# A causal mask moved from TensorE to VectorE in a two-layer decoder trunk

## The chip, the core and the metric

The program runs on one core of a Trainium2 chip. The metric is the device time of one execution in microseconds (us). Three runs of the kernel before gave 2209.25, 2209.4 and 2209.67 us; their median is 2209.4 us. The engines are named as in the profile: PE is TensorE's matrix products, PEld its weight loads, DVE is VectorE, ACT is ScalarE, POOL is GpSimd, SP is the engine that issues most of the transfers.

## What is computed

Two layers over 256 tokens of width 2048, in float32. Each layer has a token mixer (one input projection that feeds eight heads of differential attention, an RG-LRU and a gated linear attention, then one output projection) and a SwiGLU feed-forward part. The part that matters here is the attention:

```
s = jnp.einsum('bhmqd,bhmkd->bhmqk', q_blk, kh)          # m = 0, 1: two score maps per head, d = 64
qpos = i * Q_BLOCK + jnp.arange(Q_BLOCK)                 # Q_BLOCK = 128
s = jnp.where(kpos[None, :] <= qpos[:, None], s, -jnp.inf)
p = jax.nn.softmax(s, axis=-1)
a = p[:, :, 0] - lam * p[:, :, 1]
return jnp.einsum('bhqk,bhkv->bhqv', a, vh)
```

## The kernel before

Weights stream from HBM through a ring of five `raw` tiles. Each 128x512 weight chunk is split into a high and a low part, `hilo`, by ACT (a rounding copy) and DVE (a subtraction). Every projection is then made of three products for each chunk and token half (`block`, lines 419 to 421): activation high times weight high, high times low, low times high. In the trace the products of the input projection are `in`. These run one after the other nearly without a break from the start of the kernel to its end.

Everything else (attention, LRU, gated linear attention) is written as Python generators that a planner, `Lane`, weaves in between those products. The planner keeps a clock, `lane.clk`, that is advanced by an estimated time for each product, and one such estimate for DVE and ACT each (`dve.free`, `act.free`: for DVE 0.1 us and 1.04 ns for each element of a row). A generator yields a time to wait, a tile tag that must be free, and a condition; its next instructions are written into the program when the planner's clock says that they will be ready. So the order of instructions on each engine is fixed when the program is built, and the estimates decide it; at run time each engine goes through its list in order and waits on semaphores.

The attention of head `h` in a group `g` of four heads and query tile `qt` (0 or 1) is `head(h)` inside `attention`. In order: two score products for m = 0 and 1 into `sps` (line 875; their contraction is 64 long and lies on partitions 0 to 63 for m = 0 and 64 to 127 for m = 1; each writes a PSUM bank of its own; 128 keys for `qt` 0, 256 keys for `qt` 1). Behind each of them a product of a bf16 identity `ident_b` with a bf16 tile `cmask` (0 on and under the diagonal, -1e30 above it) that accumulates the mask onto the 128 columns of the diagonal (line 877). Then DVE takes the row maximum `nm` of both maps, ACT the exponential `e` with its row sum, DVE three small steps and the difference of the maps, PE transposes it (`tpa`, line 902), ACT copies it to `aT`, PE multiplies by the values (`po`, line 912). The tag `sc`, of which there is one, is held from the score products to the exponential. Two layers, two groups, two query tiles and four heads make 32 such heads in all, 64 score products and 64 mask products. An fp32 product is two passes on PE, so that a score product is two rows of MATMUL.

Further products that the trace shows and that are of use here: `psa` (line 1106, in the gated linear attention) is a set of four fp32 products with contraction 64 and 128 columns that alternate between partitions 0 to 63 and 64 to 127 and between two PSUM banks, followed by `in` products; `psg` (line 976) is two fp32 products with contraction 128 and 256 columns. DVE and ACT operations are all recorded under line 173, the planner's helper.

Of the kernel before, what the change touches and what calls it, by code (L numbers as in the profile page):

```python
# [10 lines left out]
F32 = mybir.dt.float32  # L11
F32R = mybir.dt.float32r
BF16 = mybir.dt.bfloat16
# [3 lines left out]
ALU = mybir.AluOpType  # L17
AX = mybir.AxisListType

P = 128  # L20
# [167 lines left out]
def after(us):  # L188
    return (us, None, None)
# [3 lines left out]
def tile_hybrid_trunk(ctx, tc, x, xT, w_in, w_out, w_gu, w_down, post_norms, lams,  # L193
                      vecs, wbd, w_gup, ropes, out):
    nc = tc.nc
    PS = bass.MemoryType.PSUM
    lane = Lane()
    done = lane.done
    dve, act = Engine(lane, nc.vector, 0.1, 1.04e-3), Engine(lane, nc.scalar, 0.1, 0.83e-3)
# [10 lines left out]
    cst = ctx.enter_context(tc.tile_pool(name="cst", bufs=1))  # L210
# [9 lines left out]
    rope = cst.tile([P, 2, NT, 64], F32, tag="rope", name="rope")  # L220
    ident = cst.tile([P, P], F32, tag="ident", name="ident")
    make_identity(nc, ident)
    ident_b = cst.tile([P, P], BF16, tag="identb", name="ident_b")
    nc.gpsimd.tensor_copy(ident_b, ident)
    cmask = cst.tile([P, P], BF16, tag="cmask", name="cmask")
    nc.gpsimd.memset(cmask, 0.0)
    nc.gpsimd.affine_select(out=cmask, in_=cmask, compare_op=ALU.is_ge, fill=NEG, base=0,
                            pattern=[[-1, P]], channel_multiplier=1)
# [329 lines left out]
    def split_scaled(hi, lo, src, scale):  # L558

        if scale is None:  # L560
            act.copy(hi, src)
            dve.tensor_tensor(out=lo, in0=src, in1=hi.bitcast(F32), op=ALU.subtract)
        else:
            act.activation(hi, src, AF.Copy, scale=scale)
            dve.scalar_tensor_tensor(out=lo, in0=src, scalar=scale, in1=hi.bitcast(F32),
                                           op0=ALU.mult, op1=ALU.subtract)

    def turned(src, tag, name):

        if tag == "sc":  # L570
            tp = pp.tile([P, 2, 512], F32, tag="sc", name=name, bufs=1)[:, 0, :]
        else:
            tp = pp.tile([P, 512], F32, tag=tag, name=name, bufs=1)
        tp = tp.rearrange("p (c t) -> p c t", c=4)
        for c in range(4):
            nc.tensor.transpose(tp[:, c, :], src[:, c * P:(c + 1) * P], ident)
        lane.clk += 0.44
        return tp
# [7 lines left out]
    def wide(name, tag="rp"):  # L586
        return pm.tile([P, 512], F32, tag=tag, name=name, bufs={"rp": 3, "e": 2, "on": 1}[tag])
# [154 lines left out]
    for l in range(DEPTH):  # L742
# [93 lines left out]
        def rows(name, *needs):  # L836

            return small(name, *needs).rearrange("p a b -> p (a b)").rearrange("p (t n) -> p t n", t=NT)
# [18 lines left out]
        def attention(g, qt):  # L857


            nk = (qt + 1) * P  # L860
            rsum = pt.tile([P, 4, 2], F32, tag="rsum", name="rsum")
            ssq = pt.tile([P, 4], F32, tag="ssq", name="ssq")
            po = []

            def head(h):
                prev = (l, g, qt, h - 1) if h else (l, g, 0, 3) if qt else (l, g - 1, 1, 3)
                yield 0.3, None, lane.has((l, "q", g), (l, "k", g), (l, "v", g), (l, "small"), (prev, "s"))
                yield 0.0, "sc", lambda: lane.use["e"] < 2
                done[(l, g, qt, h), "s"] = True
                lane.use["e"] += 1  # L870
                qT, kT, v = tiles[l, "q", g], tiles[l, "k", g], rows((l, "v", g))
                sps = pp.tile([P, 2, 512], F32, tag="sc", name="sps", bufs=1)
                for m in range(2):
                    r0 = slice(64 * m, 64 * m + 64)
                    nc.tensor.matmul(sps[:, m, :nk], qT[r0, h, qt * P:(qt + 1) * P],
                                     kT[r0, h, :nk], start=True, stop=False)
                    nc.tensor.matmul(sps[:, m, qt * P:nk], ident_b, cmask, start=False, stop=True)
                lane.clk += 0.55 if qt == 0 else 0.98
                yield after(0.3)
                nm = pt.tile([P, 2], F32, tag="nm", name="nm")  # L880
                dve.tensor_reduce(out=nm, in_=sps[:, :, :nk], axis=AX.X, op=ALU.max, negate=True)
                yield dve.through()
                e = wide("e", "e").rearrange("p (m k) -> p m k", m=2)
                esum = pt.tile([P, 2], F32, tag="esum", name="esum")
                for m in range(2):
                    act.activation(e[:, m, :nk], sps[:, m, :nk], AF.Exp, bias=nm[:, m:m + 1],
                                         accum_out=esum[:, m:m + 1])
                act.drops("sc")
                yield act.through()
                dve.reciprocal(rsum[:, h, :], esum)  # L890
                yield NOW
                ncf = pt.tile([P, 1], F32, tag="ncf", name="ncf")
                dve.scalar_tensor_tensor(out=ncf, in0=esum[:, 0:1], scalar=nlam,
                                               in1=rsum[:, h, 1:2], op0=ALU.mult, op1=ALU.mult)
                yield NOW
                dve.scalar_tensor_tensor(out=e[:, 0, :nk], in0=e[:, 1, :nk], scalar=ncf,
                                               in1=e[:, 0, :nk], op0=ALU.mult, op1=ALU.add)
                yield dve.through(W_SM, "tr", lambda: lane.use["aT"] < 2)
                lane.use["aT"] += 1
                tp = pp.tile([P, 2, P], F32, tag="tr", name="tpa", bufs=1)  # L900
                for kt in range(qt + 1):
                    nc.tensor.transpose(tp[:, kt, :], e[:, 0, kt * P:(kt + 1) * P], ident)
                lane.use["e"] -= 1
                lane.clk += 0.11 * (qt + 1)
                aT = pt.tile([P, 2, P], F32, tag="aT", name="aT", bufs=2)
                act.copy(aT[:, :qt + 1, :], tp[:, :qt + 1, :])
                act.drops("tr")
                yield act.through(W_AT, ("o" if h == 0 else None), lane.has((prev, "av")))
                if h == 0:
                    po.append(pp.tile([P, 4, P], F32, tag="o", name="po", bufs=1))  # L910
                for kt in range(qt + 1):
                    nc.tensor.matmul(po[0][:, h, :], aT[:, kt, :], v[:, kt, h * P:(h + 1) * P],
                                     start=(kt == 0), stop=(kt == qt))
                lane.use["aT"] -= 1
                done[(l, g, qt, h), "av"] = True
                lane.clk += 0.22 * (qt + 1)
                yield after(0.3)
                junk = pt.tile([P, 512], F32, tag="junk", name="junk", bufs=1)[:, :P]
                act.activation(junk, po[0][:, h, :], AF.Square, accum_out=ssq[:, h:h + 1])
                yield act.through()  # L920
                done[(l, g, qt, h), "end"] = True

            def norm():
                yield 0.0, None, lane.has(*(((l, g, qt, h), "end") for h in range(4)))
                r0sq = pt.tile([P, 4], F32, tag="r0sq", name="r0sq", bufs=2)
                dve.tensor_tensor(out=r0sq, in0=rsum[:, :, 0], in1=rsum[:, :, 0], op=ALU.mult)
                rr = pt.tile([P, 4], F32, tag="rr", name="rr", bufs=2)
                yield NOW
                yield from rsqrt(rr, ssq, 4, 1.0 / P, pre=r0sq)
                dve.tensor_tensor(out=rr, in0=rr, in1=rsum[:, :, 0], op=ALU.mult)  # L930
                yield NOW
                on = wide("on", "on")
                dve.tensor_tensor(out=on.rearrange("p (h d) -> p h d", h=4), in0=po[0],
                                        in1=rr[:, :, None].to_broadcast([P, 4, P]), op=ALU.mult)
                dve.drops("o")
                yield dve.through(0.25, "tr")
                tp = turned(on, "tr", name="tpo")
                sl = slice(qt * P, (qt + 1) * P)
                split_scaled(yh[:, 4 * g:4 * g + 4, sl], yl[:, 4 * g:4 * g + 4, sl], tp, subw)
                dve.drops("tr")  # L940
                done[l, "y", g, qt] = True

            done[(l, -1, 1, 3), "s"] = done[(l, -1, 1, 3), "av"] = True
            for h in range(4):
                lane.add(10 + 2 * g + qt + h / 8, head(h))
            lane.add(9, norm())
# [555 lines left out]
```

## Time and profile before

| | |
|---|---|
| median of 3 runs | 2209.4 us |
| the profiled execution | 2209.7 us |
| its span, first to last instruction | 2208.0 us |
| PE busy | 2182.3 us, 99% of the span |
| DVE busy | 1801.3 us, 82% |
| ACT busy | 1368.3 us, 62% |
| mean rate of the transfers | 212 GB/s |
| granted TensorE clock, mean | 0.999 |

A row of the timeline gives the start, the duration, the engine, the line, the operation, what it writes and reads, the shape and a count. Where rows of one kind follow without idle time they are merged: `x2` with 0.48 us means that the first began and the last ended 0.48 us apart. PE's rows overlap, since matmuls are pipelined: an `in` product has a row of 0.39 us, and the next one starts 0.22 us behind it. What a product takes from the engine is therefore read from the distance between ends (start plus duration) of neighbours and not from its own duration.

### The profile page before, as it was taken

Reading aid. Unit: us, or ns where it says so; the run is one execution under the profiler, and the core shown is the slowest. Engines: PE = TensorE matmul, PEld = TensorE weight load, DVE = VectorE, ACT = ScalarE, POOL = GpSimd, SP = SyncE. Lnnn points to the kernel's source line nnn. Section 1 sums busy time; section 2 is a strip of 40 time slices with the busy share of each in tenths; the row PEclk is TensorE's granted clock in tenths of the full one; section 3 lists DMA queues with packets and bytes.
Section 4 is the critical chain, followed back from the end, with each engine's and each line's share of the span. In section 5 each row is a group of like instructions: output and inputs, shape, how many; then the busy total and the mean of one; then the engine's idle time right before and its main releaser. Section 6 shows DMA issues by size and latency. Waiting matters only on the chain.

```text
span 2208.0 us, 30990 instructions
## 1 busy us (share of the span) xinstructions
PE 2182.3 (99%) x10116; PEld 1782.8 (81%) x10116; DVE 1801.3 (82%) x3341; ACT 1368.3 (62%) x2713; POOL 96.2 (4%) x129
## 2 busy tenths in 40 slices
PE   8999999999999999999999999999999999999998
PEld 7777878887888888888877778788878888888886
DVE  6666865898999999999786668658989999999985
ACT  6455755776666666666564557556666666666663
POOL 0000000000000000000000000000000000000000
PEclk9999999999999999999999999999999999999999
DMA  8553646677877777777644537466777887777774
GB/s 289 183 156 105 197 162 217 198 224 222 252 246 240 240 242 237 243 234 247 216 149 150 171 92 217 156 216 200 221 231 244 250 250 239 240 235 242 235 240 138
DMA packets 202722, 467.32 MB, mean 212 GB/s; under 512 B 16416, under 2 KB 27200, under 8 KB 202560
## 3 DMA queue, kind: packets, MB, share of 16 engines
q1 hardware_dynamic: 186880, 434.93, 59.5%
q0 software_dynamic: 15104, 29.37, 7.9%
q8 instruction: 79, 1.29, 0.2%
q10 hardware_dynamic: 576, 1.05, 0.1%
q14 instruction: 83, 0.68, 0.1%
HBM read 463.18 MB, written 2.10 MB: 211 GB/s over the span
## 4 chain that ended last, share of the span: by engine, by line
PE 90%; DVE 6%; DMA 1%; ACT 1%; issue 1%; SPq 0%; DVEq 0%; ACTq 0%
PE in L419 6%; PE down L419 6%; PE down L421 6%; PE in L421 6%; PE down L420 6%; PE in L420 6%; PE gu_q L456 5%; PE gu_q L455 5%; PE gu_q L454 5%; PE gu_p L454 5%; PE gu_p L456 5%; PE gu_p L455 5%; DVE hilo L173 3%; PE op L419 3%; PE op L421 3%; PE op L420 3%
## 5 line engine op out<-in xcount | busy, mean ns | idle before, releaser
L173 DVE TENSOR_TENSOR hilo<-raw,hilo 128x512 fp32r<-128x512 f32 (+1 forms) x1472 | 954.4, 675 | 288.0 <-ACT hilo L173 283.2
L173 ACT CAST hilo<-raw 128x512 fp32r<-128x512 f32 (+1 forms) x1472 | 853.9, 614 | 274.8 <-PE gu_x L456 65.4
L173 ACT CAST hilo<-t 128x512 fp32r<-128x512 f32 x384 | 231.2, 621 | 151.2 <-DVE t L173 103.4
L419 PE MATMUL in<-hilo,hh 128*128 128x512 f32 (+1 forms) x768 | 301.0, 392 | 6.0 <-ACT hilo L173 6.0
L421 PE MATMUL in<-hilo,hl 128*128 128x512 f32 (+1 forms) x768 | 287.6, 374 | 0.8 <-DVE hl L173 0.8
L420 PE MATMUL in<-hilo,hh 128*128 128x512 f32 (+1 forms) x768 | 287.0, 374 | 0.6 <-DVE hilo L173 0.6
L419 PE MATMUL down<-hilo,hid 128*128 128x512 f32 x704 | 276.9, 393 | 4.4 <-DVE c_c L173 3.6
L421 PE MATMUL down<-hilo,hid 128*128 128x512 f32 x704 | 274.7, 390 | 1.0 <-DVE hid L173 1.0
L420 PE MATMUL down<-hilo,hid 128*128 128x512 f32 x704 | 274.2, 389 | 0.0
L173 DVE TENSOR_TENSOR hilo<-t,hilo 128x512 fp32r<-128x512 f32 x384 | 247.8, 684 | 2.6 <-ACT hilo L173 2.2
L419 PEld LDWEIGHTS in<-hilo,hh 128*128 128x128 f32 x768 | 145.3, 189 | 30.8 <-ACT hilo L173 6.4
L456 PE MATMUL gu_q<-hilo,hl 128*128 128x512 f32 x432 | 168.2, 389 | 0.0
L454 PE MATMUL gu_q<-hilo,hh 128*128 128x512 f32 x432 | 168.2, 389 | 0.0
L455 PE MATMUL gu_q<-hilo,hh 128*128 128x512 f32 x432 | 168.2, 389 | 0.0
L421 PEld LDWEIGHTS in<-hilo,hl 128*128 128x128 f32 x768 | 144.6, 188 | 27.4 <-DVE hl L173 1.3
L420 PEld LDWEIGHTS in<-hilo,hh 128*128 128x128 f32 x768 | 145.3, 189 | 22.5 <-DVE hilo L173 1.9
L419 PEld LDWEIGHTS down<-hilo,hid 128*128 128x128 f32 x704 | 132.2, 188 | 35.7 <-DVE c_c L173 4.9
L421 PEld LDWEIGHTS down<-hilo,hid 128*128 128x128 f32 x704 | 132.2, 188 | 29.4 <-DVE hid L173 1.8
L420 PEld LDWEIGHTS down<-hilo,hid 128*128 128x128 f32 x704 | 132.3, 188 | 26.5
L323 POOL DMA_DIRECT2D t<-in_w_gu_dram x96 | 82.8, 867 | 1189.3 <-DMA t<-in_w_gu_dram 1177.6
L173 DVE TENSOR_TENSOR t<-t,raw 128x512 f32<-128x512 f32 x192 | 131.3, 684 | 0.0
L454 PE MATMUL gu_p<-hilo,hh 128*128 128x512 f32 x320 | 125.0, 391 | 3.3 <-DVE hid L173 3.3
(241 smaller groups left out, 3364.9 us busy)
## 6 DMA issues: line engine op xcount, KB each, us to landing
raw<-in_w_gu_dram SPq DMA_DIRECT2D x352, 512.0 KB, 4.8
raw<-in_w_down_dram SPq DMA_DIRECT2D x176, 512.0 KB, 5.2
raw<-in_w_in_dram SPq DMA_DIRECT2D x159, 512.0 KB, 4.3
raw<-in_w_out_dram SPq DMA_DIRECT2D x64, 512.0 KB, 4.8
t<-in_w_gu_dram SPq DMA_DIRECT2D x96, 256.0 KB, 3.4
t<-in_w_gu_dram POOLq DMA_DIRECT2D x96, 256.0 KB, 6.5
raw<-in_w_in_dram SPq DMA_DIRECT2D x32, 264.0 KB, 2.9
gain<-in_post_norms_dram POOLq DMA_DIRECT2D x16, 256.0 KB, 4.3
```

The lines of the kernel that those rows point to most:

```text
L173: return getattr(self.engine, name)(*args, **kwargs)
L323: nc.gpsimd.dma_start(out=o, in_=pieces[i + 1][:, 1, :], accum_op=ALU.add)
L419: nc.tensor.matmul(acc[t], ah, hi, start=(i == 0), stop=False)
L420: nc.tensor.matmul(acc[t], ah, lo, start=False, stop=False)
L421: nc.tensor.matmul(acc[t], al, hi, start=False, stop=(i == last))
L454: nc.tensor.matmul(acc, a[0], hi, start=start, stop=False)
L455: nc.tensor.matmul(acc, a[0], lo, start=False, stop=False)
L456: nc.tensor.matmul(acc, a[1], hi, start=False, stop=stop)
```

## The change

The mask becomes a float32 tile. The bf16 identity and its copy on POOL go. The score products close their accumulation themselves, the mask products go, and DVE adds the mask in place in PSUM to the diagonal 128 columns of both maps by one instruction, ahead of the row maximum. The planner's figure for the PE time of a head's scores is 0.10 us smaller, and its DVE account is charged for the addition by its usual rule (0.1 us and 1.04 ns for each of 256 elements, 0.37 us).

```
-    ident_b = cst.tile([P, P], BF16, tag="identb", name="ident_b")
-    nc.gpsimd.tensor_copy(ident_b, ident)
-    cmask = cst.tile([P, P], BF16, tag="cmask", name="cmask")
+    cmask = cst.tile([P, P], F32, tag="cmask", name="cmask")
     nc.gpsimd.memset(cmask, 0.0)
     nc.gpsimd.affine_select(out=cmask, in_=cmask, compare_op=ALU.is_ge, fill=NEG, base=0,
                             pattern=[[-1, P]], channel_multiplier=1)
...
                 for m in range(2):
                     r0 = slice(64 * m, 64 * m + 64)
                     nc.tensor.matmul(sps[:, m, :nk], qT[r0, h, qt * P:(qt + 1) * P],
-                                     kT[r0, h, :nk], start=True, stop=False)
-                    nc.tensor.matmul(sps[:, m, qt * P:nk], ident_b, cmask, start=False, stop=True)
-                lane.clk += 0.55 if qt == 0 else 0.98
+                                     kT[r0, h, :nk], start=True, stop=True)
+                lane.clk += 0.45 if qt == 0 else 0.88
                 yield after(0.3)
+                dve.tensor_tensor(out=sps[:, :, qt * P:nk], in0=sps[:, :, qt * P:nk],
+                                  in1=cmask[:, None, :].to_broadcast([P, 2, P]), op=ALU.add)
                 nm = pt.tile([P, 2], F32, tag="nm", name="nm")
                 dve.tensor_reduce(out=nm, in_=sps[:, :, :nk], axis=AX.X, op=ALU.max, negate=True)
```

## Rows read from the trace of the kernel before

**Rows 1.** Busy time by stage: the start, four attention stages; columns PE PEld DVE ACT POOL.

```profile
0.00:40.00 40.00, 33.77 (x139) 27.05 (x140) 24.69 (x51) 29.56 (x64) 2.64 (x15) 1.00 0.97 331
...
76.00:136.00 60.00, 59.94 (x284) 44.88 (x284) 39.11 (x103) 31.90 (x94) 0.00 (x0) 1.00 0.44 130
160.00:230.00 70.00, 70.00 (x349) 54.06 (x348) 43.55 (x119) 40.73 (x117) 1.64 (x2) 1.00 0.34 94
1174.00:1234.00 60.00, 59.94 (x284) 44.87 (x283) 39.16 (x103) 31.86 (x94) 0.00 (x0) 1.00 0.43 124
1258.00:1328.00 70.00, 70.00 (x349) 54.06 (x348) 43.59 (x119) 40.78 (x118) 1.49 (x2) 1.00 0.34 94
sum 260.00, PE 259.87 PEld 197.86 DVE 165.41 ACT 145.26 POOL 3.13; mean PE 64.97 PEld 49.47 DVE 41.35 ACT 36.32 POOL 0.78
```

**Rows 2.** PE's waits over the whole span: us in total, times, longest.

```profile
PE in L419 <- ACT hilo L173: 6.0, 2, 5.8
PE down L419 <- DVE c_c L173: 3.6, 8, 0.8
PE gu_p L454 <- DVE hid L173: 3.3, 2, 1.6
PE down L421 <- DVE hid L173: 1.0, 2, 0.5
PE in L421 <- DVE hl L173: 0.8, 1, 0.8
PE down L419 <- ACT hid L173: 0.8, 2, 0.4
PE in L420 <- DVE hilo L173: 0.6, 2, 0.4
PE tpx L576 <- DVE hl L173: 0.6, 1, 0.6
```

**Rows 3.** Timeline of PE and DVE, a head of query tile 0.

```profile
76.96 0.39 PE L421 MATMUL in<-hilo,hl 128*128 128x512 f32 x1
...
77.28 0.48 PE L875 MATMUL sps<-s,s 64*128 64x128 f32 x2
...
77.70 0.23 PE L877 MATMUL sps<-cmask,ident_b 128*128 128x128 bf16 x1
...
77.86 0.48 PE L875 MATMUL sps<-s,s 64*128 64x128 f32 x2
...
78.27 0.23 PE L877 MATMUL sps<-cmask,ident_b 128*128 128x128 bf16 x1
...
78.31 0.47 PE L419 MATMUL in<-hilo,hh 128*128 128x512 f32 x1
...
78.54 0.42 DVE L173 TENSOR_REDUCE nm<-sps 128x2 f32<-128x256 f32 x1
```

**Rows 4.** Timeline of PE, a head of query tile 1.

```profile
94.56 0.40 PE L421 MATMUL in<-hilo,hl 128*128 128x512 f32 x1
94.89 0.70 PE L875 MATMUL sps<-s,s 64*128 64x256 f32 x2
95.52 0.23 PE L877 MATMUL sps<-cmask,ident_b 128*128 128x128 bf16 x1
95.68 0.70 PE L875 MATMUL sps<-s,s 64*128 64x256 f32 x2
...
96.35 0.47 PE L419 MATMUL in<-hilo,hh 128*128 128x512 f32 x1
```

**Rows 5.** Timeline of PE, four 64-row products of the gated linear attention.

```profile
276.38 0.39 PE L421 MATMUL in<-hilo,hl 128*128 128x512 f32 x1
276.69 0.71 PE L1106 MATMUL psa<-s 64*128 64x128 f32 x8
277.34 0.50 PE L419 MATMUL in<-hilo,hh 128*128 128x512 f32 x1
```

**Rows 6.** Timeline of PE, fp32 passes on all 128 rows: 128 columns, then 256.

```profile
97.11 0.27 PE L902 MATMUL tpa<-ident,e 128*128 128x128 f32 x1
...
128.73 0.38 PE L902 MATMUL tpa<-ident,e 128*128 128x128 f32 x2
...
211.95 0.39 PE L421 MATMUL in<-hilo,hl 128*128 128x512 f32 x1
212.18 1.02 PE L976 MATMUL psg<-s,wg 128*128 128x256 f32 x4
```

**Rows 7.** Groups of DVE instructions by shape: count, busy us, mean ns, idle before.

```profile
L173 DVE TENSOR_TENSOR hilo<-raw,hilo 128x264 fp32r<-128x264 f32 x64 | 23.9, 414 | 15.7 <-ACT hilo L173 15.7
...
L173 DVE TENSOR_REDUCE nm<-sps 128x2 f32<-128x512 f32 x16 | 11.0, 686 | 1.9 <-PE sps L877 1.9
...
L173 DVE TENSOR_REDUCE nm<-sps 128x2 f32<-128x256 f32 x16 | 6.8, 424 | 2.9 <-PE sps L877 2.9
...
L173 DVE SCALAR_TENSOR_TENSOR e<-e,ncf 128x128 f32<-128x128 f32 x16 | 5.6, 352 | 0.6
```

**Rows 8.** Timeline of DVE and PEld, the step from `e` to its transpose.

```profile
127.83 0.48 DVE L173 SCALAR_TENSOR_TENSOR e<-e,ncf 128x256 f32<-128x256 f32 x1
...
128.50 0.37 PEld L902 LDWEIGHTS tpa<-ident,e 128*128 128x128 f32 x2
```

## The prediction

> **What bounds the kernel now.** I read the busy time by stage first, because the share over the whole span mixes stages. In the four attention stages PE is busy for 259.9 of 260 us [rows 1]; DVE is busy for 165.4 and ACT for 145.3 of them, so DVE has 94.6 us to spare there. A busy 259.9 also says that PE stands still for 0.1 us there; in the first 40 us of the kernel it is 6.2 [rows 1]. Next, PE's waits, 16.7 us in the whole run: the 6.0 of the first line is that start, the `down`, `gu_p` and `tpx` lines are the feed-forward part and its approach; no line is for `sps`, `tpa` or `po`, none for a transfer, and what else the input projection waits is one wait of 0.8 us and two of 0.6 in sum [rows 2]. So in the attention the order on PE sets the time, and a microsecond taken off PE there is a microsecond off the end, as long as the inputs of the products behind it come as much earlier. They can: transfers run at 94 to 130 GB/s in these stages against the 212 of the whole run, and DVE and ACT idle for a third and more [rows 1]. Last, the timeline around one head, because a merged or pipelined row doesn't tell what a product costs; the distance between ends does.
>
> **What the mask costs on PE.** Query tile 0 [rows 3]: the last `in` product ahead of the scores ends at 76.96 + 0.39 = 77.35, the first one behind them at 78.31 + 0.47 = 78.78. The head's scores with that one `in` product take 1.43 us. Query tile 1 [rows 4]: from 94.56 + 0.40 = 94.96 to 96.35 + 0.47 = 96.82, 1.86 us. Now what passes cost by themselves. Two fp32 passes of 128 columns on all rows take 0.38 us against 0.27 for one, so a pass more is 0.11; four of 256 columns end 0.86 us after the `in` product ahead of them (213.20 less 212.34), 0.215 each, with nothing on top [rows 6]. So in query tile 0 four passes are 0.44 and an `in` product some 0.23 (the starts of neighbours); 0.76 of the 1.43 us are left for two mask products that stream 128 columns each. Most of that is no streaming: it is the engine going back and forth between 64-row products and full-row ones.
>
> The trace holds a model of the scores without a mask: `psa`, four 64-row products in a row, halves alternating, each half with a bank of its own, as in `sps`. From the `in` product ahead (276.38 + 0.39 = 276.77) to the end of the one behind (277.34 + 0.50 = 277.84) it is 1.07 us [rows 5], less than the 1.43 of two masked score products, though it streams twice the passes. Its eight passes lie within 0.71 us; one after the other they would need 0.27 + 7 x 0.11 = 1.04. So the two halves run side by side, and four slots of 0.11 do the eight passes. Into the 1.07 the way into the 64-row form and out of it is already counted.
>
> Scores without mask, query tile 0: two slots fewer than `psa`, 1.07 - 2 x 0.11 = 0.85 us; saved 1.43 - 0.85 = 0.58. Query tile 1: two passes of 256 columns span 0.70 where two of 128 span 0.48 [rows 3, 4], so 0.85 + 0.22 = 1.07; saved 1.86 - 1.07 = 0.79. Sixteen heads of each: 16 x 0.58 + 16 x 0.79 = 9.3 + 12.6 = **21.9 us**. (A few heads are followed by a transpose and not by an `in` product; I price them the same.)
>
> Bounds of this term. If the halves did not overlap, two more slots come back: 0.85 + 0.22 = 1.07 and 1.07 + 2 x 0.215 = 1.50, saved 0.36 and 0.36, in all 11.5 us. If no switching went at all but the mask's own place, 0.16 us from a mask's start to the next score's [rows 3, 4], 64 x 0.16 = 10.2, or by a bare pass of 0.11 [rows 6] 7.0. From the other side: should leaving the scores cost no more than the mask's leaving does now, 0.28 (78.78 less 78.50) [rows 3] and not `psa`'s 0.44 (277.84 less 277.40) [rows 5], the sum grows by 32 x 0.16 = 5.1. I take 21.9, since `psa` has the same shape, halves and banks as the scores of query tile 0.
>
> **What the addition costs.** No row shows DVE writing PSUM. Bounds: two-input DVE instructions take 0.35 us at 128 elements, and one that reads 512 elements of PSUM takes 0.69; the nearest in kind and length, 264 elements, takes 0.414 [rows 7]. I take 0.42: 32 x 0.42 = 13.4 us of DVE, and between 11.3 and 22.0. All of it fits into the 94.6 us that DVE idles in these stages [rows 1], and PE waits for none of it as long as the steps behind it come in time. If that cover were gone, it would be 13.4 us on the end.
>
> [...]
>
> **What it does to a head's chain.** The wait on the scores moves from the maximum to the addition; it is the same wait (DVE waited 2.9 and 1.9 us in all for `sps` there [rows 7]), and behind it in DVE's queue stand, as now, `hilo` subtractions for products some way ahead. The addition puts 0.42 us ahead of `nm`, but the scores end earlier: now the chain from the first score product to the end of the maximum is 78.54 + 0.42 - 77.28 = 1.68 us [rows 3]; then PE's part is 0.71 - 0.22 = 0.49 [rows 5], DVE starts some 0.04 later as it does now, and 0.42 + 0.42 follow: 1.37. So in real time the chain gets no longer. In the planner's time it gets 0.37 longer and the scores 0.10 shorter, so the exponential, the transpose and `po` are written a little later between the `in` products, which gives them more room. The tightest place now is a transpose whose weights are loaded 0.19 us after `e` is done (128.50 less 128.31) [rows 8].
>
> **Edits at nothing.** The fp32 `cmask`, the missing `ident_b` and its copy are set-up on POOL, ahead of any use by some 75 us. No transfer is added. `raw` transfers are issued when a `hilo` subtraction frees a buffer; those follow PE and move up with it.
>
> **The sum.** The profiled execution took 2209.7 us, span 2208.0 and 1.7 around it. Less 21.9 is 2187.8. Each layer's order of instructions is woven anew from the first head on, and some product will stand where its input is a little late; I put 0.5 us on each layer for it, of the size of the one wait of 0.8 [rows 2]: 2188.8. The median of the runs is 0.3 below the profiled execution, so **2188.5 us**, 0.95% faster.
>
> **Rivals.**
> A, the forecast: switches go, halves overlap. Chance 0.70.
> B, the halves run one after the other: saved 11.5, less 1 for the order, 2198.9. For it: an accumulating pair in `sps` has never been seen without a mask between. Against it: `psa`. Chance 0.13.
> C, only the mask's own place goes and the switching stays in another form: 7.0 to 10.2, 2199 to 2202. Against it: `psa` and `psg`, which show no cost beyond passes and, for `psa`, one way in and out. Chance 0.05.
> C0, the mask's streaming is mostly hidden by what its neighbours do anyway, and its removal is worth less than C's lower end, half of it say: 3.5, 2206, no change that can be told. Against it: 0.16 us from a mask's start to the next product's [rows 3]. Chance 0.02. [...]
> D, the new order gives back part: PE's waits outside the start are 16.7 - 6.6 = 10.1 us [rows 2]; were the new order to add as much, 2198. Chance 0.05.
> F, the addition lies on the path in full, because DVE's list and not PE's becomes what the `in` products wait for: 2209.4 - 21.9 + 13.4 = 2201. Against it: the 94.6 us that DVE idles in the stages [rows 1]. Chance 0.02.
> E, the other side: the in-order queues. The addition stands in DVE's list until the scores are done, `e` comes later, and PE, in order too, stops at each transpose. To eat the gain PE has to lose 21.9 / 32 = 0.69 us at every head, on top of the 0.19 it has at the tightest: from about 0.9 us more delay of `e` at each head it decides. At 1.0 us PE would lose 0.8 a head, 3.7 us more than it gains: 2213, and with 0.3 us more still at each head 2223. Against it: the chain above gets shorter. Chance 0.03.
>
> **Range and chances.** The likeliest is A, 2188.5; its own range is 2184 (the lower bound of leaving) to 2192 (3 us of new waits). Taking in B, and D up to its full size, the range is 2184 to 2199; what is left out is C, C0, F, E and the ends of A and B, below 2 in 10. A measurement here tells 0.2%, 4.4 us, from no change. A, B, C, D and F are beyond it: faster 0.95, same 0.02 (C0), slower 0.03 (E).
>
> **What would show it.** In the profile after: 1.43 and 1.86 us between `in` products become 0.85 and 1.07, with the four score passes of a head as one row of about 0.49 and 0.71 us; the addition a DVE row of about 0.42 us, 32 times; `sps` as DVE's releaser at the addition and not at the maximum; PE still busy through the stages, each attention stage shorter by 5 us or so; the feed-forward part unchanged. Wrong would be: score rows of 0.7 us for query tile 0 (B), PE waits on `e`, `aT` or `hilo` of some us in the stages (D, E), or a gain that is there in the stages and gone by the output projection.

## The result, and the profile after

The changed kernel takes 2192.98 us (median of four runs, 2192.14 to 2193.08) against 2209.39 for the kernel before: ratio 0.9923, 95% interval 0.9911 to 0.9935. It is faster by 16.4 us, 0.74%; 2188.5 and 20.9 were forecast. The profiled execution has a span of 2191.3 us, 16.7 less than before.

First the timeline of PE around a head of each query tile, the places of [rows 3] and [rows 4]:

```profile
77.35 0.39 PE L419 MATMUL in<-hilo,hl 128*128 128x512 f32 x1
77.67 0.49 PE L873 MATMUL sps<-s,s 64*128 64x128 f32 x4
78.09 0.50 PE L417 MATMUL in<-hilo,hh 128*128 128x512 f32 x1
...
95.35 0.40 PE L419 MATMUL in<-hilo,hl 128*128 128x512 f32 x1
95.67 0.70 PE L873 MATMUL sps<-s,s 64*128 64x256 f32 x4
96.31 0.50 PE L417 MATMUL in<-hilo,hh 128*128 128x512 f32 x1
```

From end to end of the `in` products it is now 78.59 - 77.74 = 0.85 us and 96.81 - 95.75 = 1.06, in place of 1.43 and 1.86. The four passes of a head share one row of 0.49 or 0.70 us, not more than the two passes of one half took before.

Next DVE, in the groups by shape [rows 7], and its timeline at the first head; [rows 3] has the same `nm` before:

```profile
L173 DVE TENSOR_TENSOR sps<-sps,cmask 128x256 f32<-128x256 f32 x32 | 13.6, 426 | 0.0
L173 DVE TENSOR_REDUCE nm<-sps 128x2 f32<-128x512 f32 x16 | 11.1, 692 | 0.6
L173 DVE TENSOR_REDUCE nm<-sps 128x2 f32<-128x256 f32 x16 | 6.8, 425 | 0.6
```

```profile
78.32 0.69 DVE L173 TENSOR_TENSOR hilo<-raw,hilo 128x512 fp32r<-128x512 f32 x1 [4.97 <-ACT hilo L173]
78.93 0.42 DVE L173 TENSOR_TENSOR sps<-sps,cmask 128x256 f32<-128x256 f32 x1
79.39 0.42 DVE L173 TENSOR_REDUCE nm<-sps 128x2 f32<-128x256 f32 x1
```

The addition takes 0.426 us, 13.6 for all 32. Its idle time is 0.0: DVE never waits at it for the scores. It is the other way round; the scores are done at 77.67 + 0.49 = 78.16 and the addition starts 0.77 us later, right behind a subtraction (the two rows overlap by 0.08 us). Over the 32 heads of the trace it starts 0.47 to 6.65 us after the last score pass. Before, the maximum started 0.04 us after the last mask product at 22 of the 32.

Last PE's waits [rows 2]:

```profile
PE in L417 <- ACT hilo L173: 6.1, 2, 5.3
PE down L417 <- DVE c_c L173: 3.6, 8, 0.8
PE gu_p L452 <- DVE hid L173: 3.3, 2, 1.6
PE tpa L901 <- DVE e L173: 1.2, 2, 0.6
PE po L911 <- ACT junk L173: 1.1, 2, 0.6
PE down L419 <- DVE hid L173: 1.0, 2, 0.5
PE tpo L574 <- DVE on L173: 0.8, 2, 0.4
```

The three lines for `tpa` on `e`, `po` on ACT and `tpo` on DVE are new. Such lines show idle time between PE's modelled rows only. A fuller account adds up, over all PE rows of one kind, the distance from the end of the row ahead to the end of this one, so that every microsecond of the span belongs to one kind. Worked out from the traces (us; the kernels e1 to e4 follow below; each kind that is left out differs by less than 0.3 between before and after):

```
kind               before   after  after-before |    e1      e2      e3      e4
sps, mask included  43.67   16.88    -26.79     |  23.84   17.23   16.88   16.88
in, 512 columns    454.47  458.70     +4.23     | 454.61  458.87  458.78  458.75
tpa                  5.26    6.87     +1.61     |   5.85   10.53    6.63    6.05
po                  11.57   12.87     +1.30     |  11.59   12.49   11.62   12.88
tpo                  3.50    4.72     +1.22     |   3.50    3.50    3.49    4.71
tpog                 1.75    2.17     +0.42     |   1.75    1.75    1.75    2.28
op                 175.05  176.36     +1.31     | 175.03  175.05  175.05  176.38
all                2207.99 2191.33   -16.66     | 2188.80 2192.88 2187.18 2190.48
```

The first two lines belong together (the way out of the scores is counted at the `in` product behind them): -22.6 us. The five lines below give back 5.9.

### The profile page after: what moved, and what is told of

The parts are those of the page before. It is cut to its first block, busy times and chain, and to the rows that moved or that the text cites. A ratio compares the mean times of both kernels' runs of the same rounds, so it can differ in the third digit from the quotient of the medians.

```text
span 2191.3 us, 30890 instructions
## 1 busy us (share of the span) xinstructions
PE 2162.1 (99%) x10052; PEld 1769.5 (81%) x10052; DVE 1814.0 (83%) x3373; ACT 1372.6 (63%) x2715; POOL 96.1 (4%) x128
## 3 DMA queue, kind: packets, MB, share of 16 engines
q10 hardware_dynamic: 576, 1.05, 0.1%
## 4 chain that ended last, share of the span: by engine, by line
PE 88%; DVE 8%; ACT 1%; issue 1%; DMA 1%; SPq 0%; DVEq 0%; ACTq 0%
PE in L417 6%; PE down L417 6%; PE down L419 6%; PE down L418 6%; PE in L419 6%; PE in L418 6%; PE gu_q L454 5%; PE gu_q L452 5%; PE gu_q L453 5%; PE gu_p L452 5%; PE gu_p L454 5%; PE gu_p L453 5%; DVE hilo L173 4%; PE op L419 2%; PE op L417 2%; PE op L418 2%
```

## The experiments

Two questions: what was it on PE that cost so much, and where did the 5.9 us come from. Each ratio is to the kernel before on the same chip.

**e1: both masks on TensorE, behind both scores.** The kernel before with one line moved:

```
                 for m in range(2):
                     nc.tensor.matmul(sps[:, m, :nk], ..., start=True, stop=False)
+                for m in range(2):
                     nc.tensor.matmul(sps[:, m, qt * P:nk], ident_b, cmask, start=False, stop=True)
```

> The kernel before, with one edit: both score products of a head come first and the two mask products behind them, all still on TensorE; the order of everything else and the planner's figures stay. Theory S (switching): what a mask product costs between two score products is the way out of the 64-row form and back in, so that this order alone wins most of the gain without any work for VectorE. The passes of the scores then end 0.42 us (query tile 0) or 0.63 us (query tile 1) behind the in product ahead; the first mask adds 0.16, the second 0.05 to 0.16, the next in product 0.28: 0.91 to 1.02 and 1.12 to 1.23 us in place of 1.43 and 1.86. Sum over 16 heads of each 16.8 to 20.2 us: 2189 to 2193 us. Theory M (the mask products themselves): 64 products are still there, so the time stays within 2 us of 2209.4.

Measured: 2190.91 us, ratio 0.9915 (0.9901 to 0.9928). The timeline of PE, a head of each query tile:

```profile
76.91 0.39 PE L421 MATMUL in<-hilo,hl 128*128 128x512 f32 x1
77.22 0.49 PE L875 MATMUL sps<-s,s 64*128 64x128 f32 x4
77.65 0.28 PE L878 MATMUL sps<-cmask,ident_b 128*128 128x128 bf16 x2
77.74 0.48 PE L419 MATMUL in<-hilo,hh 128*128 128x512 f32 x1
...
92.46 0.40 PE L421 MATMUL in<-hilo,hl 128*128 128x512 f32 x1
92.79 0.70 PE L875 MATMUL sps<-s,s 64*128 64x256 f32 x4
93.42 0.29 PE L878 MATMUL sps<-cmask,ident_b 128*128 128x128 bf16 x2
93.52 0.47 PE L419 MATMUL in<-hilo,hh 128*128 128x512 f32 x1
```

From end to end 78.22 - 77.30 = 0.92 and 93.99 - 92.86 = 1.13 us: of the 0.58 and 0.80 that the change wins at a head, 0.51 and 0.73 are won with all 64 mask products kept, in the same order of everything else. Theory M falls. What cost the time was a full-row product between two 64-row ones; in their new place the two masks cost 0.07 us a head more than none.

The gain has two parts, by the rows of before. There the second score product ends 0.41 us behind the mask ahead of it in query tile 0 (78.34 less 77.93 [rows 3]) and 0.63 in query tile 1 (96.38 less 95.75 [rows 4]); in e1 its passes lie beside those of the first. At 0.11 and 0.215 us a pass, an estimated 0.22 and 0.43 of that is the two halves running side by side, and the other 0.2 is the way back into the 64-row form. A further 0.1 is the second mask, which ended 0.16 us behind the product ahead of it and now ends 0.06 behind. The way in does not hang on the masks' bf16 type: the first score product, behind an f32 `in` product, takes the same 0.41 us (77.76 less 77.35).

**e2: the change in the order of before.**

```
-                lane.clk += 0.45 if qt == 0 else 0.88
+                lane.clk += 0.55 if qt == 0 else 0.98
-                dve.tensor_tensor(out=sps[:, :, qt * P:nk], ...
+                nc.vector.tensor_tensor(out=sps[:, :, qt * P:nk], ...
```

> The changed kernel's work (mask added by VectorE, no mask products) in the order of the kernel before: the planner's figure for the scores is put back to 0.55 and 0.98 us and the addition is not charged to its VectorE account, so that each engine's list is that of before with 64 products left out and 32 additions put in. Theory O (order): the 5.4 us that the changed kernel lost are waits of the new order, and the additions are hidden: gain 22.0 us, 2187.4 us, with PE's waits on tpa, po, tpo and the output projection as before. Theory V (VectorE): the additions delay what PE waits for whatever the order: 2192 to 2194 us.

Measured: 2194.66 us, ratio 0.9932 (0.9919 to 0.9946), slower than the change. Theory O as I put it falls: the addition is not hidden in the old order; V is the nearer one here. In its trace PE, DVE and ACT have the lists of before, instruction for instruction, but for the masks left out and the additions put in. In the account `tpa` takes 5.3 us more than before. Its timeline at one head of group 1, DVE and PE:

```profile
206.40 0.49 DVE L173 SCALAR_TENSOR_TENSOR e<-e,ncf 128x256 f32<-128x256 f32 x1
...
207.00 0.20 PEld L901 LDWEIGHTS tpa<-ident,e 128*128 128x128 f32 x2 [0.71 <-issue]
207.03 0.41 PE L901 MATMUL tpa<-ident,e 128*128 128x128 f32 x2 [0.30 <-DVE e L173]
```

PE stands at the transpose until `e`, done at 206.89, has come. At 16 of the 32 heads the transpose starts 0.15 us behind `e`, as close as it comes in any of these traces; in the kernel before none starts closer than 0.4 us.

**e3: as e2, without the addition** (the two lines of the addition taken out).

> As the run in the order of before, but the additions are left out as well: no causal mask is applied at all. Theory O: as that run within 1 us, 2187 us. Theory V: 2187 us too, and thus 5 us under that run.

Measured: 2188.68 us, ratio 0.9905 (0.9892 to 0.9919). The 32 additions cost 2194.66 - 2188.68 = 6.0 us of their 13.6 in the old order, as theory V has it. The time lies 1.7 us over the 2187 of both theories: the account has new waits of 1.4 us at `tpa` and 0.3 at `tp_lx`, although the order is that of before and nothing was added.

**e4: the change's own order, without the addition.**

```
-                dve.tensor_tensor(out=sps[:, :, qt * P:nk], ...
+                dve.free = max(dve.free, lane.clk) + 0.1 + 1.04e-3 * 2 * P
```

> The changed kernel's order, instruction for instruction, without the 32 additions (no causal mask is applied): the planner is still charged for them. Theory O: the waits stay, since they come from the order: 2191 to 2193 us. Theory V: they go with the additions: 2187 to 2188 us.

Measured: 2191.93 us, ratio 0.9919 (0.9905 to 0.9933): theory O's range, 3.2 us over e3 with the same instructions in another order. The intervals of the two ratios overlap, but the runs do not (2188.43 to 2189.74 and 2191.67 to 2192.22), and the account places the difference: 4.3 us more at `po`, `tpo`, `tpog` and `op`, 1.1 less at `tpa` and `tp_lx`. So the loss has two parts, and they trade. The order that the charge weaves costs 3.2 us more than the old one; in it the additions cost about 1 us (2192.98 - 2191.93 = 1.05, by the account 0.8 at `tpa`; the runs of the two kernels touch, so that the size is not sure). In the old order they cost 6.0. The room of the transposes fits this: in the change 2 of the 32 start as close as 0.15 us behind `e`, in e2 16 do.

What the new order does is seen at the end of the mixer. PE's timeline in the changed kernel; `tpog` turns the last rows of the gated linear attention for the products behind it:

```profile
314.30 0.39 PE L419 MATMUL op<-hilo,yl 128*128 128x512 f32 x1
314.54 0.81 PE L574 MATMUL tpog<-ident,ong 128*128 128x128 f32 x4
315.10 0.48 PE L417 MATMUL op<-hilo,yh 128*128 128x512 f32 x1
...
316.12 0.50 PE L417 MATMUL op<-hilo,yh 128*128 128x512 f32 x1
316.46 0.40 PE L418 MATMUL op<-hilo,yh 128*128 128x512 f32 x1
316.91 0.50 PE L419 MATMUL op<-hilo,yl 128*128 128x512 f32 x1
```

Counted in the traces, 54 products of the output projection stood ahead of this transpose before, 72 now. The next ones need its result: PE's weight load waits 0.52 us for `yh` at 316.12 and 0.49 for `yl` at 316.91. The last head of group 1 moved too. Its scores start at 202.39 before, ahead of the first gate product `psg` at 212.18 [rows 6]; at 216.97 in the changed kernel, behind the gates.

**e5: the addition twice**, in the change's order (the same line once more through `nc.vector`, not charged).

> The changed kernel in its own order, with the addition issued twice in a row for each head; the second is not charged to the planner. The mask is then added twice, which masks the same places. Theory L (the lists): an addition delays the head's steps behind it by its own 0.43 us, and PE pays only where the transpose's room is smaller. In the trace of the changed kernel the first transpose pass of the heads starts 0.15 (one that waits) to over 8 us after e is done; with 0.43 us more, the heads with less than 0.58 lose some 0.1, 0.2, 0.2 and 0.4 us in each group of layer 0, 1.1 us a layer: 2195.2 us. Theory P (the addition lies on the path in full): 32 x 0.43 more, 2206.7. Theory H (it is hidden): 2193.0.

Measured: 2195.07 us, ratio 0.9933 (0.992 to 0.9947): theory L to 0.1 us, and `tpa` takes 9.00 us against 6.87 in the account. It also comes at the heads where I had put it: in layer 0 the four transposes with the least room take 0.16, 0.24, 0.19 and 0.46 us more than in the change, for 0.1, 0.2, 0.2 and 0.4. The largest wait, 1.08 us at the last head of group 1, holds the 0.62 that this head waits in the change already.

```profile
227.84 0.48 DVE L173 SCALAR_TENSOR_TENSOR e<-e,ncf 128x256 f32<-128x256 f32 x1
228.44 0.20 PEld L903 LDWEIGHTS tpa<-ident,e 128*128 128x128 f32 x2 [1.26 <-issue]
228.47 0.30 PE L903 MATMUL tpa<-ident,e 128*128 128x128 f32 x1 [1.08 <-DVE e L173]
```

**e7 and e8: other figures for the planner**, the addition charged as in the change.

```
-                lane.clk += 0.45 if qt == 0 else 0.88
+                lane.clk += 0.62 if qt == 0 else 0.83      # e7
+                lane.clk += 0.55 if qt == 0 else 0.98      # e8
```

> The changed kernel with the planner told what the scores take from PE by the trace, 0.62 and 0.83 us in place of 0.45 and 0.88; the addition is charged as in the change. Theory O1: the waits of the new order come from the planner taking the scores of query tile 0 for too short; they go, and the time falls to 2188 to 2190. Theory O2: any new figure weaves another order whose waits are a draw: 2188 to 2195, PE's work the same to within 0.5 us.

> The changed kernel with only the planner's figure for the scores put back to 0.55 and 0.98 us; the addition stays charged. One part of the change undone. Theory O1: too short a figure is the fault, a longer one takes some of the waits away: 2190 to 2192. Theory O2: another draw, 2188 to 2195. Against the run in the old order without the charge, 2194.7, it tells what the charge alone does.

Measured: e7 2192.09 us, ratio 0.9921 (0.9907 to 0.9934); e8 2192.0, 0.9921 (0.9907 to 0.9935). O1 falls with e7: true figures for PE don't take the waits away (e8 lies at the upper end of its range, but that is theory O2's range too). For O2's wide draw there is no sign either; three orders with the charge lie within 1 us of one another. In all three `po` takes 12.85 to 12.87 us, `tpo` 4.59 to 5.05, `tpog` 2.16 to 2.17 and `op` 176.35 to 176.38, and 72 products of the output projection stand ahead of the transpose shown under e4. Without the charge (e2, e3) it is 54, and `tpo`, `tpog` and `op` are as before. e8 and e2 differ by the charge alone. So the waits at these three come with the charge for the addition, and the figure for PE only moves about the rest. `po` is no such clear case: 11.62 in e3, but 12.49 in e2.

**e9 and e10: the change and e1 side by side** on one chip.

> The changed kernel again, beside the kernel with both masks behind the scores, on the same chip: 2193 us. If the two differ by what their PE accounts say (the changed kernel's scores take 2.8 us less, its waits 5.2 us more), the other one is 2.1 us faster; if the orders of 2192.98 and 2190.91 were chance between chips, they lie within 0.5 us.

> The kernel before with both mask products behind both score products, beside the changed kernel on the same chip: 2190.5 to 2191.5 us, some 2 us under it by the PE accounts.

Measured: 2192.5 us (2192.18 to 2192.77), ratio 0.992 (0.9906 to 0.9934), and 2190.87 (2190.61 to 2191.61), 0.9913 (0.9899 to 0.9927). The kernel with both masks on TensorE, one line moved, is 1.6 us under the change, nearer to the 2.1 of the accounts than to the 0.5 of chance; their runs don't overlap. It is less than the 0.2% that I took a measurement to tell, and the intervals of the ratios overlap, so I claim no more than that e1 is not the slower one. The change's scores take 2.9 us less of PE (-26.79 + 4.23 against -19.83 + 0.14), its waits 5.2 more.

## Why the prediction was right, and where it was off

**The switching (forecast A): right.** 0.85 and 1.07 us a head were worked out from `psa`; 0.85 and 1.06 were measured, 21.9 us forecast, 22.6 in the account. B (halves in series, 1.07 and 1.50), C and C0 (the mask's own place) are out, by the change's rows and by e1. By the estimate under e1 the halves side by side are worth 16 x (0.22 + 0.43) = 10.4 us of it, and the rest is the masks and the ways between the forms. The way back into the 64-row form costs some 0.2 us a head by that estimate, and the four passes of two halves share a row of 0.49 us. What TensorE does in the 0.2 us, no row shows.

**The price of the addition: right.** 0.42 forecast, 0.426 measured, and no wait of PE is on the addition. F, where it would have lain on the path in full, is out: about 1 us of 13.6 in the change's order, 6.0 in the old one.

**"In real time the chain gets no longer": wrong.** I had DVE start 0.04 us after the scores and the maximum end 1.37 us after they began, down from 1.68. At the first head it is 79.39 + 0.42 - 77.67 = 2.14. I shortened the chain by what PE became faster, but DVE takes its list in order, and in it a `hilo` subtraction stands ahead, tied to ACT (the row at 78.32, 4.97 us idle before it). Before, that subtraction and the scores ended at nearly the same time, which looked like a wait on the scores alone; DVE's timeline of the kernel before, one row ahead of the `nm` of [rows 3]:

```profile
77.93 0.69 DVE L173 TENSOR_TENSOR hilo<-raw,hilo 128x512 fp32r<-128x512 f32 x1 [4.63 <-ACT hilo L173]
```

It ends at 78.62, the masked scores at 78.50. When the scores took 0.49 us in place of 1.22, nothing was won behind them, and the addition's 0.42 came on top. The idle time says the same: DVE waited 1.9 and 2.9 us for the scores at the two groups of `nm` [rows 7], all of it at 10 of the 32 heads, and waits 0.0 at the addition; the 0.6 and 0.6 now ahead of `nm` are some 0.04 us a head between the addition and the maximum. The sign that I named, `sps` as DVE's releaser at the addition, did not come. At the 16 heads of query tile 0 the mean from the first score pass to the end of `nm` is 1.69 us before, 1.63 in e3 (old order, no addition) and 2.14 in the change: of the 0.73 us that PE became faster there, 0.06 reached the end of the maximum in e3. e3 against e2 shows what the addition costs where the planner doesn't know of it.

**"0.5 us on each layer" for the new order: the term that was mis-sized.** It measured 5.9 us in PE's account for both layers together, where the sum has 1.0. By the runs, 3.2 of it is the order (e4 against e3) and about 1 the additions in it (e4); the remaining 1.6 is as much as e3 loses already, when only PE's part gets shorter (in the change it no longer lies where it does in e3). The 4.9 us too much, less a PE gain 0.7 larger than forecast, are 4.2 of the 4.5 by which 2188.5 missed; the other 0.3 was taken off for the median, which here lies 0.06 under the profiled execution. So the time is 1 us above A's own range (2184 to 2192), within the whole one. It is rival D at a bit over half its size, on top of A. E was wrong in size, though its mechanism is the one in e2: in the change the largest wait at a transpose is 0.6 us and the sum at `tpa` 1.6 over 32 heads, where E needed 0.69 at each.

That the charge delays the last head and the gated linear attention because a head holds the tag `sc` for longer in the planner's time is read from the code; no run shows it apart. Why `po` waits longer in the charged orders was not taken apart.

## What to carry to other kernels

When small-contraction products are mixed with full ones, group them by form: here that won 0.51 and 0.73 us a head with all 64 mask products kept (e1), and the four passes of two halves shared a row of 0.49 or 0.70 us. Moving one line, with all the work kept, won as much (2190.91 us) as moving the work to another engine (2192.98). Read the price of a product from the distance between its neighbours' ends, and look for a place in the same trace where the form stands without the operation in question. Before letting a chain become shorter because one link does, look at what stands ahead of the next link in its engine's list: here, of the 0.73 us by which the scores of query tile 0 became shorter, 0.06 came through (e3). A list woven from estimates gave back part of the gain as waits both where the added step was not accounted for (6.0 us, e2 against e3) and where accounting for it moved other work late (3.2 us, e4 against e3).

## What the runs showed of the hardware that was not expected

The price of a bf16 mask product depended on its neighbour: between 64-row products a start-to-start distance of 0.16 us and, by the estimate under e1, a way back of some 0.2 us behind it; as the second of two in a row, 0.05 to 0.06 (two share 0.28 to 0.29 us in e1 where one has 0.23). An fp32 addition by DVE that reads and writes PSUM in place takes 0.426 us for 256 elements, 1 to 3% over what 264 elements take between SBUF tiles (0.420 in the same trace, 0.414 before [rows 7]).
